# The attention's maxima: two heads as products on half the rows each

## Chip, cores, metric

The kernel runs on one core of a Trainium2 chip. The metric is the device time of one execution in microseconds. Three runs of the kernel before took 2360.37, 2365.2 and 2371.74 us; their median is 2365.2.

## The reference

One layer computes a prompt of 2048 tokens and a sample group of 8 x 4 tokens: RMSNorm, one input projection, then native sparse attention (NSA) beside a gated DeltaNet, and one output projection. What the change touches is the attention of the prompt. It has 8 query heads of 64 dimensions in 2 groups of 4; each group shares one key/value head. Three branches are softmaxed by themselves and summed under gates: compressed blocks, the 8 selected blocks of 64 keys, and a window of 512 keys.

```python
def window_banded(q, k, v):
    ...
    s = jnp.einsum('bnqhgd,bnkhd->bhgnqk', q_b, kw).astype(jnp.float32) * (NSA_HEAD_DIM ** -0.5)
    ...
    p = jax.nn.softmax(jnp.where(m, s, MASK_VALUE), axis=-1)
```

A softmax subtracts a maximum per query and head, and that maximum may be approximate, since it cancels. The selected branch does the same over the chosen blocks.

## The kernel before, in words

The program runs through input projection, gated DeltaNet (`gdn`, with the compression of keys beside it), attention (`nsa`) and output projection. A scheduler of the framework writes the order of every engine at build time: it goes through the recorded instructions by priority and by its own estimate of when operands and buffers are ready. PE, the tensor engine, then takes its products in exactly that order.

**Units.** `nsa` works in 8 units: 4 blocks of 512 queries (`qs`) times 2 groups of heads (`h`). While the scores of one unit are streamed (`stream`), `prepare` computes the maxima of the next, some of its steps after each step of the stream. For the first unit `prepare` runs alone beside the end of the DeltaNet's recurrence.

**Operands.** Queries and keys are split into a high and a low part. `QHL` [128, 4, 512] holds a group's 4 heads: rows 0 to 63 the high part (16 rotated dimensions `rh`, 48 others `qh`), rows 64 to 127 the low part (`rl`, `ql`). `KHH` holds the keys' high part twice, in rows 0 to 63 and 64 to 127. A product over all 128 rows is thus (high + low) x high. `load_q` (L1213 for each DMA) loads QHL with four DMAs on SP's queue.

**Maxima.** For each of the unit's 4 query tiles `s` and 4 heads `g`, `smax` (L1374) multiplies 128 queries with up to 512 keys into a PSUM tile `psm`, adds the causal mask of the last tile by a second product, the bf16 identity times the bf16 mask `neglow` (L1376), and VectorE reduces each 64 keys to a maximum in `bm` (L1377). `wmax` (L1389 to L1391) does this for the window into `psw`, in one or two pieces, always with a mask. `wmax0` (L1397 to L1400) takes all 4 heads at the window's far edge into `psv`. The PSUM tiles come from `pM` with 3 buffers, shared with `psc`, `psi`, `tsel`, `L`, `B` and others.

**Stream.** For each key tile and pair of heads `score` makes two products per head (L1440 on QHL's 128 rows, L1441 on 98 rows) into `pss`, ScalarE exponentiates them (L1482), and two products with the values (L1573) go to the halves of `O`: the even head to columns 0 to 63, the odd one to 64 to 127. `B` (L1528) has 24 rows. `gdn_setup` and L695 use the same bf16 identity and mask for the DeltaNet's decay.

```python
mm = nc.tensor.matmul(O[64 * gg:64 * gg + 64, c0:c1], val, W[j][gg][:, c0:c1], ..., tile_position=(0, 64 * gg))
```

`tile_position` names the first row and column of the part of the array that a product uses.

Of the kernel before, what the change touches and what calls it, by code (L numbers as in the profile page):

```python
# [104 lines left out]
class K:  # L105
# [15 lines left out]
    def setup(self):  # L121
# [3 lines left out]
        self.identb = self.const.tile([128, 128], BF16, name="identb")  # L125
        nc.vector.tensor_copy(self.identb, self.ident)
# [28 lines left out]
    def setup2(self):  # L155
        nc = self.nc
        self.masks = {}
        with self.pool(name="set", bufs=1, side="right") as sp:
            for n in ("negtri", "neglow"):
                f = sp.tile([128, 128], F32, tag="f", name="f_" + n)  # L160
                nc.sync.dma_start(f, self.i[n][:, 0:128])
                self.masks[n] = self.const.tile([128, 128], BF16, name=n)
                nc.vector.tensor_copy(self.masks[n], f)
# [399 lines left out]
    def gdn_setup(self, cp, bank):  # L563
# [6 lines left out]
        negtri = cp.tile([128, 512], BF16, name="negtri")  # L570
        nc.vector.tensor_copy(negtri, ntf)
        nc.sync.dma_start(ntf, i["headind"])
# [64 lines left out]
    def gdn(self):  # L637
        nc, tc, i, o = self.nc, self.tc, self.i, self.o
        with self.gst as st:
# [51 lines left out]
            def build(n):  # L691
# [3 lines left out]
                nc.tensor.matmul(psd, self.identb, negtri, start=True, stop=False)  # L695
# [510 lines left out]
    def nsa(self):  # L1206
        nc, tc, i, o = self.nc, self.tc, self.i, self.o
        with ExitStack() as st:
# [38 lines left out]
            def load_q(qs, h):  # L1247
# [8 lines left out]
                dma(QHL[0:16], qv(self.rh))  # L1256
                dma(QHL[16:64], qv(self.qh, 16))
                dma(QHL[64:80], qv(self.rl))
                dma(QHL[80:128], qv(self.ql, 16))
# [17 lines left out]
            def X(shape, name):  # L1277
                return pM.tile(shape, F32, tag="m", name=name)
# [10 lines left out]
            tri4 = wk.tile([128, 4, 128], BF16, name="tri4", bufs=1)  # L1289
            nc.gpsimd.tensor_copy(tri4, self.masks["negtri"].unsqueeze(1).to_broadcast([128, 4, 128]))  # L1290
# [6 lines left out]
            def prepare(u):  # L1297
# [71 lines left out]
                def smax(s, g, a):  # L1369
                    qt = 4 * qs + s  # L1370
                    b = min(a + 4, qt + 1)
                    diag = b == qt + 1
                    ps = X([128, 512], "psm")
# [3 lines left out]
                    nc.vector.tensor_reduce(out=bm[:, s, g, 2 * a:2 * b], in_=ps[:, 0:128 * (b - a)].rearrange("p (n k) -> p n k", k=64), axis=AX.X, op=ALU.max)  # L1377
                    busy["d"] += 0.1 + 0.14 * (b - a)

                def wmax(s, g):  # L1380
# [3 lines left out]
                    lhs = QHL[:, g, 128 * s:128 * s + 128]  # L1384
                    ps = X([128, 512], "psw")
                    parts = [(x, y) for x, y in ((a, min(e, 4 * qs)), (max(a, 4 * qs), e)) if x < y]
                    for x, y in parts:
                        last = y == e
                        nc.tensor.matmul(ps[:, 128 * (x - a):128 * (y - a)], lhs, key(KHH, 1, h, x, y), start=True, stop=not last)  # L1389
                    nc.tensor.matmul(ps[:, 128 * (qt - a):128 * (qt - a) + 128], self.identb, self.masks["neglow"], start=False, stop=True)  # L1390
                    nc.vector.tensor_reduce(out=ww[:, g, s, 0:1], in_=ps[:, 0:128 * (e - a)], axis=AX.X, op=ALU.max)  # L1391
                    busy["d"] += 0.1 + 0.14 * (e - a)
# [22 lines left out]
                for s in range(4):  # L1415
                    for g in range(4):
                        B += [lambda s=s, g=g, a=a: smax(s, g, a) for a in range(0, 4 * qs + s + 1, 4)]
                        B += [lambda s=s, g=g: wmax(s, g)]
# [18 lines left out]
            prepare.steps = lambda u: 16 + 32 + 16 * u["qs"] + (4 if u["qs"] else 0)  # L1437
# [615 lines left out]
```

## Time and profile before

| | |
|---|---|
| median of three runs | 2365.2 us |
| profiled execution | 2365.14 us |
| span of its trace | 2363.4 us |
| PE busy | 2183.8 us (92%) |
| VectorE (DVE) busy | 1280.0 us (54%) |
| ScalarE (ACT) busy | 796.7 us (34%) |
| GpSimd (POOL) busy | 763.3 us (32%) |
| granted clock of PE, mean | 0.958 |

PE's busy time is that of its products, whose ends are modelled and overlap; its weight loads are a row of their own (PEld). What a product costs is read from the starts of the products around it. The attention is the stretch from about 1239 to 2065 us.

### The profile page before, as it was taken

What the parts mean: (1) busy time and instruction counts of PE and PEld (TensorE: products, weight loads), DVE (VectorE), ACT (ScalarE), POOL (GpSimd) and SP (SyncE); (2) the same over time, 40 slices, a digit from 0 to 9 for tenths busy, and PEclk for the clock granted to TensorE, in tenths of its full rate; (3) what the DMA queues carried; (4) which work ended last, traced back from release to release, by engine and by line L of the source; (5) the groups of instructions that cost most, each with busy time, mean ns of one, the idle gap of its engine ahead of it and who ended that gap; (6) DMA issues with size and microseconds to landing.
All of it is one profiled execution on the core that took longest, in us unless ns stands there. A gap on an engine that the chain in (4) does not pass through costs nothing. (4 is left out here: it accounts for less than half of the span.)

```text
span 2363.4 us, 36125 instructions
## 1 busy us (share of the span) xinstructions
PE 2183.8 (92%) x13338; PEld 1668.8 (71%) x13340; DVE 1280.0 (54%) x2660; ACT 796.7 (34%) x1688; POOL 763.3 (32%) x957
## 2 busy tenths in 40 slices
PE   4999989999999899996793899999999999999998
PEld 4999888999999888996682455455455453477765
DVE  4300135566521266566551578687768787844542
ACT  4411224332214133453351324334343444522221
POOL 2104211111100004512141246455464655422742
PEclk9999999999999899998796989998999999999999
DMA  8432331124442464546638342232122102384652
GB/s 244 130 83 93 100 106 63 59 69 81 119 145 87 141 179 128 157 128 150 138 104 169 62 83 52 35 67 53 39 47 39 28 6 60 93 241 145 197 189 94
DMA packets 304467, 248.12 MB, mean 105 GB/s; under 512 B 106039, under 2 KB 260835, under 8 KB 301987
## 3 DMA queue, kind: packets, MB, share of 16 engines
q1 hardware_dynamic: 282923, 194.53, 32.2%
q0 software_dynamic: 7424, 33.56, 4.2%
q10 hardware_dynamic: 13944, 17.72, 2.6%
q8 instruction: 105, 1.72, 0.3%
q14 instruction: 71, 0.58, 0.1%
HBM read 173.60 MB, written 74.42 MB: 105 GB/s over the span
## 5 line engine op out<-in xcount | busy, mean ns | idle before, releaser
L1583 POOL TENSOR_TENSOR pt<-pt 128x512 f32<-128x512 f32 (+3 forms) x332 | 320.6, 977 | 371.4 <-DVE pt L1492 178.9
L1482 ACT ACTIVATE pt<-pss 128x512 f32<-128x512 f32 (+3 forms) x544 | 254.8, 494 | 383.9 <-PE pss L1441 204.4
L1573 PE MATMUL O<-pt,V 128*64 128x512 f32 (+3 forms) x1088 | 243.1, 527 | 10.9 <-DVE pt L1492 10.9
L1377 DVE TENSOR_REDUCE bm<-psm 128x8 f32<-128x512 f32 (+3 forms) x320 | 189.6, 603 | 66.3 <-PE psm L1374 49.5
L1440 PE MATMUL pss<-qhl,khh 128*128 128x512 f32 (+3 forms) x544 | 218.6, 407 | 1.2 <-ACT pt L1482 0.6
L1440 PEld LDWEIGHTS pss<-qhl,khh 128*128 128x128 f32 x544 | 105.4, 194 | 135.9 <-issue 97.2
L1441 PE MATMUL pss<-qhm,klm 98*128 98x512 f32 (+3 forms) x544 | 191.8, 361 | 5.4 <-DMA qhl<-rl 4.0
L261 PE MATMUL ps<-xhi,whi 128*128 128x416 f32 x880 | 191.0, 359 | 2.5 <-ACT sb L514 2.5
L261 PE MATMUL ps<-xhi,wlo 128*128 128x416 f32 x880 | 189.7, 355 | 0.0
L261 PE MATMUL ps<-xlo,whi 128*128 128x416 f32 x880 | 187.6, 354 | 0.0
L261 PEld LDWEIGHTS ps<-xhi,whi 128*128 128x128 f32 x880 | 166.7, 191 | 15.9 <-issue 4.7
L261 PEld LDWEIGHTS ps<-xlo,whi 128*128 128x128 f32 x880 | 166.1, 189 | 2.1
L261 PEld LDWEIGHTS ps<-xhi,wlo 128*128 128x128 f32 x880 | 165.7, 189 | 1.9
L1492 DVE TENSOR_TENSOR pt<-pt,caps 128x128 f32<-128x128 f32 x349 | 138.1, 415 | 21.1 <-ACT pt L1482 19.9
L1374 PE MATMUL psm<-khh,qhl 128*128 128x512 f32 (+3 forms) x320 | 129.0, 416 | 18.0 <-DMA qhl<-ql 11.5
L1583 DVE TENSOR_TENSOR pt<-pt 128x512 f32<-128x512 f32 (+3 forms) x148 | 122.8, 839 | 32.7 <-PE O L1573 17.4
L466 DVE SCALAR_TENSOR_TENSOR acc<-cx,wc,acc 128x416 f32<-128x416 f32 (+1 forms) x180 | 124.1, 690 | 4.6
L1441 PEld LDWEIGHTS pss<-qhm,klm 98*128 98x128 f32 x544 | 106.4, 197 | 17.0 <-DMA qhl<-rl 4.9
L1573 PEld LDWEIGHTS O<-pt,V 128*64 128x64 f32 x1088 | 55.9, 137 | 85.6 <-issue 33.3
L239 DVE TENSOR_TENSOR wlo<-wraw,whi 128x1024 fp32r<-128x1024 f32 x30 | 35.7, 1223 | 146.1 <-ACT whi L238 133.9
L1391 DVE TENSOR_REDUCE ww<-psw 128x1 f32<-128x512 f32 (+3 forms) x128 | 80.9, 632 | 51.7 <-PE psw L1390 50.9
L1374 PEld LDWEIGHTS psm<-khh,qhl 128*128 128x128 f32 x320 | 62.0, 198 | 57.2 <-issue 16.6
(506 smaller groups left out, 4150.3 us busy)
## 6 DMA issues: line engine op xcount, KB each, us to landing
kq<-qkvt SPq DMA_DIRECT2D x64, 256.0 KB
qkvt<-acc SPq DMA_DIRECT2D x60, 208.0 KB
wraw<-w_in SPq DMA_DIRECT2D x24, 512.0 KB
xt<-x_prompt SPq DMA_DIRECT2D x16, 512.0 KB
m<-mx SPq DMA_DIRECT2D x16, 512.0 KB
x<-x_prompt ACTq DMA_DIRECT2D x16, 512.0 KB
out<-y SPq DMA_DIRECT2D x16, 512.0 KB
qh<-hi SPq DMA_DIRECT2D x20, 208.0 KB
```

The costliest lines, as they stand in the source:

```text
L239: nc.vector.tensor_tensor(out=wlo[:, :, c:c + m], in0=raw, in1=whi[:, :, c:c + m].bitcast(F32), op=ALU.subtract)
L261: nc.tensor.matmul(ps, x, y, start=(k == 0), stop=(k == 23))
L466: nc.vector.scalar_tensor_tensor(acc[:, :n], cx[:, j:j + n], wc[:, j, c:c + 1], acc[:, :n], op0=ALU.mult, op1=ALU.add)
L1374: nc.tensor.matmul(ps[:, 0:128 * (b - a)], QHL[:, g, 128 * s:128 * s + 128], key(KHH, 0, h, a, b), start=True, stop=not diag)
L1377: nc.vector.tensor_reduce(out=bm[:, s, g, 2 * a:2 * b], in_=ps[:, 0:128 * (b - a)].rearrange("p (n k) -> p n k", k=64), axis=AX.X, op=ALU.max)
L1391: nc.vector.tensor_reduce(out=ww[:, g, s, 0:1], in_=ps[:, 0:128 * (e - a)], axis=AX.X, op=ALU.max)
L1440: nc.tensor.matmul(ps, lhs1, r1, start=True, stop=False)
L1441: nc.tensor.matmul(ps, lhs2, r2, start=False, stop=True)
L1482: last = nc.scalar.activation(pt[:, c0:c1], ps[:, c0:c1], AF.Exp)
L1492: last = nc.vector.tensor_tensor(out=x, in0=x, in1=caps[:, int(nm == "neglow")], op=ALU.min)
L1573: mm = nc.tensor.matmul(O[64 * gg:64 * gg + 64, c0:c1], val, W[j][gg][:, c0:c1], start=(n == 0), stop=(n == N - 1), tile_position=(0, 64 * ...
L1583: (nc.gpsimd if e == "p" else nc.vector).tensor_tensor(out=acc[gg][:, c0:c1], in0=acc[gg][:, c0:c1], in1=W[j][gg][:, c0:c1], op=ALU.add)
```

## The change

The rows of QHL are swapped for odd heads: even heads have the high part in rows 0 to 63 and the low part in 64 to 127, odd heads the other way round. KHH is the same in both halves, so the full products of the scores and of `wmax0` do not change. `smax` and `wmax` now take a pair of heads `p`: each head's product runs over its high part alone, 64 rows, at row 64 * j for head j of the pair, into a PSUM tile of its own. The low part of the queries is left out of these maxima. A dependency without a wait keeps the pair's products in the order odd, even. The identity and the masks are fp32r; `tri4` is replaced by a broadcast of `negtri`. QHL is loaded with eight DMAs, each for two heads. `prepare` has half as many steps for the maxima, each twice as large.

```diff
+        self.identr = self.const.tile([128, 128], F32R, name="identr")
+        nc.vector.tensor_copy(self.identr, self.ident)
...
+        for n in ("negtri", "neglow"):
+            self.masks[n] = self.const.tile([128, 128], F32R, name=n)
...
+        negtri = cp.tile([128, 512], F32R, name="negtri")
         nc.vector.tensor_copy(negtri, ntf)
+        nc.vector.tensor_copy(self.masks["negtri"], ntf[:, 0:128])
+        nc.sync.dma_start(ntf[:, 0:128], i["neglow"][:, 0:128])
+        nc.vector.tensor_copy(self.masks["neglow"], ntf[:, 0:128])
...
-                nc.tensor.matmul(psd, self.identb, negtri, start=True, stop=False)
+                nc.tensor.matmul(psd, self.identr, negtri, start=True, stop=False)
...
-                dma(QHL[0:16], qv(self.rh))
-                dma(QHL[16:64], qv(self.qh, 16))
-                dma(QHL[64:80], qv(self.rl))
-                dma(QHL[80:128], qv(self.ql, 16))
+                for odd in range(2):
+                    for a, r, x in ((64 * odd, self.rh, self.qh), (64 - 64 * odd, self.rl, self.ql)):
+                        dma(QHL[a:a + 16, odd::2], qv(r)[:, odd::2])
+                        dma(QHL[a + 16:a + 64, odd::2], qv(x, 16)[:, odd::2])
...
+                def both(name, ws, mask=None):
+                    t = [X([128, 512], name) for _ in range(2)]
+                    def run(p, s):
+                        first = None
+                        for n, (c, k) in enumerate(ws):
+                            for j in (1, 0):
+                                r = slice(64 * j, 64 * j + 64)
+                                mm = nc.tensor.matmul(t[j][:, c:c + k.shape[-1]], QHL[r, 2 * p + j, s], k[r], start=True, stop=not (mask is not None and n == len(ws) - 1), tile_position=(64 * j, 0))
+                                if first is not None:
+                                    tc.add_manual_dep(mm.ins, first.ins.name, mybir.DependencyInfo(mybir.DependencyClass.NoSync, mybir.DependencyReason.DATA), reason="both heads at once")
+                                first = mm
+                        if mask is not None:
+                            for j in (1, 0):
+                                nc.tensor.matmul(t[j][:, mask:mask + 128], self.identr, self.masks["neglow"], start=False, stop=True)
+                        return t
+                    return run
...
-                    nc.tensor.matmul(ps[:, 0:128 * (b - a)], QHL[:, g, 128 * s:128 * s + 128], key(KHH, 0, h, a, b), start=True, stop=not diag)
-                    if diag:
-                        nc.tensor.matmul(ps[:, 128 * (qt - a):128 * (qt - a) + 128], self.identb, self.masks["neglow"], start=False, stop=True)
+                    t = both("psm", [(0, key(KHH, 0, h, a, b))], 128 * (qt - a) if b == qt + 1 else None)(p, slice(128 * s, 128 * s + 128))
+                    for j in range(2):
+                        nc.vector.tensor_reduce(out=bm[:, s, 2 * p + j, 2 * a:2 * b], in_=t[j][:, 0:128 * (b - a)].rearrange("p (n k) -> p n k", k=64), axis=AX.X, op=ALU.max)
...
+                    t = both("psw", [(128 * (x - a), key(KHH, 1, h, x, y)) for x, y in parts], 128 * (qt - a))(p, slice(128 * s, 128 * s + 128))
...
-                    nc.tensor.matmul(ps, self.identb, tri4, start=True, stop=False)
+                    nc.tensor.matmul(ps, self.identr, self.masks["negtri"].unsqueeze(1).to_broadcast([128, 4, 128]), start=True, stop=False)
...
-            prepare.steps = lambda u: 16 + 32 + 16 * u["qs"] + (4 if u["qs"] else 0)
+            prepare.steps = lambda u: 16 + 16 + 8 * u["qs"] + (4 if u["qs"] else 0)
```

**The order, first place.** PE in the stream of the unit with `qs` 2 and `h` 1, while the maxima of `qs` 3, `h` 0 are made: unmasked maxima. `psm` are the maxima, `pss` the scores, `O` the values; `khh` is a block of 512 keys. Before:

```order
L1374 MATMUL psm<-khh_11699,qhl_11700 128x512
L1440 MATMUL pss<-qhl_11706,khh_11711 128x512
L1441 MATMUL pss<-qhm_11707,klm_11712 128x512
L1374 MATMUL psm<-khh_11705,qhl_11700 128x512
L1573 MATMUL O<-pt,V_11709 64x512 x2
L1440 MATMUL pss<-qhl_11706,khh_11711 128x384
L1441 MATMUL pss<-qhm_11707,klm_11712 128x384
L1374 MATMUL psm<-khh_11711,qhl_11700 128x512
```
The changed kernel, in the stream of the same unit (the lines of scores and values are 10 higher):

```order
L1376 MATMUL psm<-khh_11692,qhl_11693 128x512
L1450 MATMUL pss<-qhl_11699,khh_11692 128x512
L1451 MATMUL pss<-qhm_11700,klm_11695 128x512
L1450 MATMUL pss<-qhl_11699,khh_11692 128x512
L1451 MATMUL pss<-qhm_11700,klm_11695 128x512
L1583 MATMUL O<-pt,V_11696 64x512 x2
L1376 MATMUL psm<-khh_11692,qhl_11693 128x512
L1450 MATMUL pss<-qhl_11699,khh_11698 128x512
L1451 MATMUL pss<-qhm_11700,klm_11701 128x512
L1376 MATMUL psm<-khh_11698,qhl_11693 128x512 x2
L1450 MATMUL pss<-qhl_11699,khh_11698 128x512
```
A head's product stood alone between scores before. Now the two products of a pair stand apart, with four products of the scores and two of the values between the first two; the next pair stands together.

**The order, second place.** The same unit, maxima with a mask (`neglow`). Before:

```order
L1374 MATMUL psm<-khh_11715,qhl_11700 128x128
L1376 LDWEIGHTS identb
L1376 MATMUL psm<-neglow,identb 128x128
L1440 MATMUL pss<-qhl_11706,khh_11711 128x256
L1441 MATMUL pss<-qhm_11707,klm_11712 128x256
L1389 MATMUL psw<-khh_11711,qhl_11700 128x384
L1389 MATMUL psw<-khh_11715,qhl_11700 128x128
L1390 LDWEIGHTS identb
L1390 MATMUL psw<-neglow,identb 128x128
```
The changed kernel (the odd head of a pair, then the even one):

```order
L1376 MATMUL psm<-khh_11708,qhl_11693 128x128
L1382 MATMUL psm<-neglow,identr 128x128
L1450 MATMUL psr<-QRL,chh 128x512
L1451 MATMUL psr<-QRM,cxl 128x512
L1376 MATMUL psm<-khh_11708,qhl_11693 128x128
L1382 MATMUL psm<-neglow,identr 128x128
L1583 MATMUL O<-pt,V_11706 64x128 x2
```
and a few rows later, the window's pair:

```order
L1583 MATMUL O<-pt,V_11696 64x512 x2
L1538 MATMUL B<-R,ep 128x512
L1376 MATMUL psw<-khh_11704,qhl_11693 128x384 x2
L1376 MATMUL psw<-khh_11708,qhl_11693 128x128 x2
L1382 MATMUL psw<-neglow,identr 128x128 x2
```
Before, each product was followed by its mask. Now a masked pair of `psm` is split: product and mask of one head, two products of `psr`, product and mask of the other. The window's pair, in two pieces of 384 and 128 keys, stands together, and its two masks follow it.

## Rows read from the trace of the kernel before

**Rows 1.** Busy time of each engine by stretches (the header names the columns).
```profile
core 0: us, PE busy (x) PEld busy (x) DVE busy (x) ACT busy (x) POOL busy (x), PEclk, DMA share, GB/s
1119.80:1238.70 118.90, 104.50 (x1004) 87.99 (x1004) 69.10 (x207) 51.89 (x182) 37.91 (x63) 0.89 0.49 120
1238.70:2065.40 826.70, 753.01 (x3618) 392.24 (x3616) 600.18 (x1200) 312.77 (x664) 395.14 (x402) 0.94 0.28 59
1238.70:1400.00 161.30, 114.48 (x596) 64.01 (x596) 82.76 (x213) 40.96 (x100) 42.19 (x58) 0.85 0.54 109
1800.00:2065.40 265.40, 255.55 (x1175) 123.94 (x1173) 213.00 (x386) 117.78 (x241) 140.09 (x129) 0.97 0.18 45
```
**Rows 2.** PE's groups by line, 1238.7 to 2065.4 us.
```profile
L1440 PE MATMUL pss<-qhl,khh 128*128 128x512 f32 (+3 forms) x544 | 218.6, 407 | 1.2 <-ACT pt L1482 0.6
L1374 PE MATMUL psm<-khh,qhl 128*128 128x512 f32 (+3 forms) x304 | 121.9, 414 | 17.1 <-DMA qhl<-ql 11.5 <-DVE ww L1391 3.7 <-DVE bm L1377 1.6
L1389 PE MATMUL psw<-khh,qhl 128*128 128x128 f32 (+3 forms) x184 | 51.1, 342 | 0.7 <-DVE ww L1391 0.2
L1376 PE MATMUL psm<-neglow,identb 128*128 128x128 bf16 x112 | 26.3, 235 | 0.0
```
**Rows 3.** Who waited for whom, PE and its weight loads (PEld), same stretch: us, times, longest.
```profile
PE psr L1441 <- DMA QRM<-rows: 32.8, 1, 32.8
PE psm L1374 <- DMA qhl<-ql: 11.5, 6, 4.1
PEld pss L1440 <- ACT pt L1482: 31.2, 57, 0.8
PEld psm L1374 <- DVE bm L1377: 15.0, 25, 1.7
```
**Rows 4.** PE in order of time: start us, length us, then the instruction; scores and maxima.
```profile
1511.46 0.40 PE L1440 MATMUL pss<-qhl,khh 128*128 128x512 f32 x1
1511.69 0.40 PE L1441 MATMUL pss<-qhm,klm 98*128 98x512 f32 x1
1511.93 0.39 PE L1374 MATMUL psm<-khh,qhl 128*128 128x512 f32 x1
```
**Rows 5.** PE in order of time around a product on 24 rows.
```profile
1437.48 0.39 PE L1374 MATMUL psm<-khh,qhl 128*128 128x256 f32 x1
1437.71 0.23 PE L1376 MATMUL psm<-neglow,identb 128*128 128x128 bf16 x1
1437.75 0.48 PE L1440 MATMUL psr<-QRL,chh 128*128 128x512 f32 x1
1438.07 0.39 PE L1441 MATMUL psr<-QRM,cxl 98*128 98x512 f32 x1
1438.39 0.49 PE L1528 MATMUL B<-R,ep 24*128 24x512 f32 x1
1438.81 0.50 PE L1440 MATMUL pss<-qhl,khh 128*128 128x512 f32 x1
1439.14 0.40 PE L1441 MATMUL pss<-qhm,klm 98*128 98x512 f32 x1
1439.39 0.28 PE L1389 MATMUL psw<-khh,qhl 128*128 128x256 f32 x1
```
**Rows 6.** PE in order of time, from transposes to a product on 64 rows and 64 columns.
```profile
932.66 0.60 PE L1161 MATMUL tp<-ident,subh 128*128 128x128 f32 x4
932.99 0.27 PE L1161 MATMUL tp<-ident,subh 128*128 128x128 f32 x1
933.19 0.67 PE L777 MATMUL pq<-Y,A 64*64 64x64 f32 x8
```
**Rows 7.** PE in order of time, values: two heads on column halves.
```profile
1509.88 1.08 PE L1573 MATMUL O<-pt,V 128*64 128x512 f32 x4
1510.36 0.60 PE L1573 MATMUL O<-pt,V 128*64 128x512 f32 x2
1510.89 0.50 PE L1440 MATMUL pss<-qhl,khh 128*128 128x512 f32 x1
```
**Rows 8.** SP's issues of line 1213: length of one, shortest, median, longest, in ns.
```profile
L1213 SPq DMA_DIRECT2D qhl<-ql x8: 302/424/427, 1103.1 to 1824.2; - x8
```

More of the change, by code (lines that the diff above doesn't have):

```diff
@@ L124, in setup @@
         nc.sync.dma_start(self.ident, self.i["ident"])
-        self.identb = self.const.tile([128, 128], BF16, name="identb")
-        nc.vector.tensor_copy(self.identb, self.ident)
+        self.identr = self.const.tile([128, 128], F32R, name="identr")
+        nc.vector.tensor_copy(self.identr, self.ident)
         self.ones = self.const.tile([128, 128], F32, name="ones")
@@ L157, in setup2 @@
         self.masks = {}
[L158 to L163, printed above, removed]
+        for n in ("negtri", "neglow"):
+            self.masks[n] = self.const.tile([128, 128], F32R, name=n)
         self.ovl = self.const.tile([128, 32], F32, name="ovl")
@@ L569, in gdn_setup @@
         nc.sync.dma_start(ntf, i["negtri"])
-        negtri = cp.tile([128, 512], BF16, name="negtri")
+        negtri = cp.tile([128, 512], F32R, name="negtri")
         nc.vector.tensor_copy(negtri, ntf)
+        nc.vector.tensor_copy(self.masks["negtri"], ntf[:, 0:128])
+        nc.sync.dma_start(ntf[:, 0:128], i["neglow"][:, 0:128])
+        nc.vector.tensor_copy(self.masks["neglow"], ntf[:, 0:128])
         nc.sync.dma_start(ntf, i["headind"])
@@ L1288, in nsa @@
             busy = {"p": 0.0, "d": 0.0}
-            tri4 = wk.tile([128, 4, 128], BF16, name="tri4", bufs=1)
-            nc.gpsimd.tensor_copy(tri4, self.masks["negtri"].unsqueeze(1).to_broadcast([128, 4, 128]))
             caps = wk.tile([128, 2, 128], F32, name="caps", bufs=1)
@@ L1367, in sel_rows @@
                     nc.sync.dma_start(QHM[64:96, 1:4].bitcast(F32), QHM[64:96, 0:1].bitcast(F32).to_broadcast([32, 3, 512]))
-                def smax(s, g, a):
+                def both(name, ws, mask=None):
[14 more added lines that the diff above has]
+                    return run
@@ L1370, in smax @@
+                def smax(s, p, a):
                     qt = 4 * qs + s
                     b = min(a + 4, qt + 1)
-                    diag = b == qt + 1
-                    ps = X([128, 512], "psm")
-                    nc.tensor.matmul(ps[:, 0:128 * (b - a)], QHL[:, g, 128 * s:128 * s + 128], key(KHH, 0, h, a, b), start=True, stop=not diag)
-                    if diag:
-                        nc.tensor.matmul(ps[:, 128 * (qt - a):128 * (qt - a) + 128], self.identb, self.masks["neglow"], start=False, stop=True)
@@ L1377, in smax @@
-                    nc.vector.tensor_reduce(out=bm[:, s, g, 2 * a:2 * b], in_=ps[:, 0:128 * (b - a)].rearrange("p (n k) -> p n k", k=64), axis=AX.X, op=ALU.max)
-                    busy["d"] += 0.1 + 0.14 * (b - a)
-                def wmax(s, g):
+                    t = both("psm", [(0, key(KHH, 0, h, a, b))], 128 * (qt - a) if b == qt + 1 else None)(p, slice(128 * s, 128 * s + 128))
+                    for j in range(2):
+                        nc.vector.tensor_reduce(out=bm[:, s, 2 * p + j, 2 * a:2 * b], in_=t[j][:, 0:128 * (b - a)].rearrange("p (n k) -> p n k", k=64), axis=AX.X, op=ALU.max)
@@ L1382, in wmax @@
+                    busy["d"] += 2 * (0.1 + 0.14 * (b - a))
+                def wmax(s, p):
                     qt = 4 * qs + s
                     a, e = max(0, qt - 3), qt + 1
-                    lhs = QHL[:, g, 128 * s:128 * s + 128]
-                    ps = X([128, 512], "psw")
                     parts = [(x, y) for x, y in ((a, min(e, 4 * qs)), (max(a, 4 * qs), e)) if x < y]
-                    for x, y in parts:
-                        last = y == e
-                        nc.tensor.matmul(ps[:, 128 * (x - a):128 * (y - a)], lhs, key(KHH, 1, h, x, y), start=True, stop=not last)
@@ L1390, in wmax @@
-                    nc.tensor.matmul(ps[:, 128 * (qt - a):128 * (qt - a) + 128], self.identb, self.masks["neglow"], start=False, stop=True)
-                    nc.vector.tensor_reduce(out=ww[:, g, s, 0:1], in_=ps[:, 0:128 * (e - a)], axis=AX.X, op=ALU.max)
-                    busy["d"] += 0.1 + 0.14 * (e - a)
+                    t = both("psw", [(128 * (x - a), key(KHH, 1, h, x, y)) for x, y in parts], 128 * (qt - a))(p, slice(128 * s, 128 * s + 128))
+                    for j in range(2):
+                        nc.vector.tensor_reduce(out=ww[:, 2 * p + j, s, 0:1], in_=t[j][:, 0:128 * (e - a)], axis=AX.X, op=ALU.max)
@@ L1394, in wmax0 @@
+                    busy["d"] += 2 * (0.1 + 0.14 * (e - a))
                 def wmax0(s):
@@ L1415, in prepare @@
                 for s in range(4):
-                    for g in range(4):
-                        B += [lambda s=s, g=g, a=a: smax(s, g, a) for a in range(0, 4 * qs + s + 1, 4)]
-                        B += [lambda s=s, g=g: wmax(s, g)]
+                    for p in range(2):
+                        B += [lambda s=s, p=p, a=a: smax(s, p, a) for a in range(0, 4 * qs + s + 1, 4)]
+                        B += [lambda s=s, p=p: wmax(s, p)]
                     if qs:
```

## The prediction

> **What bounds the kernel now.** I read the windows of the stage first. The attention with its maxima is the stretch from 1238.7 to 2065.4 us: TensorE (PE) is busy 753.0 of 826.7 us, VectorE 600.2, ScalarE 312.8, GpSimd 395.1; in its last third PE is busy 255.6 of 265.4 us [rows 1]. So this stage goes at PE's pace, and PE takes its products strictly in the written order. The maxima are 520 products of queries with keys here (160 pairs of heads for psm, 100 for psw); the 304 + 184 of them in this stage, with their masks, are among PE's larger groups [rows 2]. Of PE's 73.7 us of idle time 32.8 are a single wait for a DMA, another 11.5 wait for the load of QHL, and the rest are short waits for ScalarE and VectorE [rows 3].
>
> The durations in PE's rows overlap, so a product's price is read from starts. In a run of products that all use the whole array, 512 columns follow each other at 0.23 us: 1511.46, 1511.69, 1511.93 [rows 4]. Call the part of the array that a product takes its layout (128, 64 or 32 rows; 128, 64 or 32 columns). **Where the layout changes the pace breaks.** B has 24 rows: psr starts 0.32 us before it instead of 0.23, B itself lasts 0.42 until the next start, and the first product after it 0.33, before the pace is back at 0.25 with the next [rows 5]. So a change first costs 0.09 us (the running product must end before anything of the new layout starts) and then 0.10 us more in the new layout (0.42 against 0.32, 0.33 against 0.23: the first weights are not loaded under the product before). Together 0.19 us per change to a layout of 128 weight columns; into O's 64 columns about half of the load, 0.14. A change to 64 rows is in the trace too, with 64 columns: four transposes start from 932.66 to 932.99, 0.11 apart, then 0.20 pass until pq [rows 6]. That is the same 0.09.
>
> **The change, part by part.**
>
> *Side by side.* The 520 products stream 198,656 columns (counted in the order), before and after. A product on 64 rows costs as much as one on 128, unless the partner on the other half runs at the same time. The trace shows column halves side by side: four products of O in 1.01 us, two of them in 0.53 [rows 7]. Row halves at 128 columns it doesn't show; bounds: full overlap or none. In the order of the changed kernel, though, the two heads mostly do not stand together: the dependency fixes that odd comes before even, not that nothing comes between. Scores, values and masks stand between them, as both places of the order above show. The half-row products form 370 stretches; 274 hold one product alone, 55 two, 28 three, 13 four. Only 41,472 columns have a partner. At 0.23 us per 512 columns that saves 18.6 us at most, 0 at least; I take 18.6, since O's halves overlap fully.
>
> *Layout changes.* Before, the maxima were whole-array products like the scores (pss) around them and changed nothing. Now each stretch is entered and left. I counted the changes of layout in the order: 672 in the stage before, 1224 after, 552 more, of them 543 to 128 weight columns. 543 x 0.19 + 9 x 0.14 = 104 us. From below: if weights for half the rows can load while other products run, only the 0.09 is left, 50 us; if a change between 128 and 64 rows at 128 columns is free, 0. From above 0.19, as B's rows are the nearest (128 columns, fewer rows). I take 104.
>
> *Masks.* 256 masks take fp32r weights instead of bf16. The bf16 mask costs 0.04 us until the next start and leaves the next load bare, 0.32 instead of 0.23 [rows 5]: 0.13. An fp32r mask of 128 columns is paced by its load, 0.11 like the transposes [rows 6]; 214 of the 256 follow a half-row product, and their bare load is already in the price of the change. So 0, with -5 to +8 as bounds (256 x -0.02 to +0.03). The 24 masks of psv and 16 of psd stand behind 512-column products that hide a load of 0.11: 0.
>
> *DMA.* QHL is loaded with 8 DMAs instead of 4 of the same bytes; an issue takes 0.42 us on SP [rows 8]. PE already waits 11.5 us in six times for QHL's last piece [rows 3], and four more issues ahead of it are up to 1.7 us in seven loads: 0 to 12, I take 2, since in the new order other products stand ahead of the first maximum. The two mask copies from ntf, and tri4's copy that falls away on GpSimd, have no follower on PE's path in this stage: 0.
>
> *Before the stage.* From 1119.8 to 1238.7 the first maxima run beside the end of the recurrence; PE is busy 104.5 of 118.9 us [rows 1] at small chained products. The changes of layout grow from 97 to 156 there: 59 x 0.19 = 11 us at most; the chain sets the end, I take 3.
>
> *Buffers.* A pair holds two of pM's three PSUM buffers. VectorE has 227 us to spare in the stage [rows 1], and PE waits 15.0 us for psm's reductions now [rows 3]. A slower PE leaves them more time, so no new wait is counted.
>
> **The sum.** In the stage 104 - 19 = +85 us of PE at the full clock. The granted clock is 0.94 [rows 1], so +91. Of the 41 us of idle time that are not the one long wait, a slower PE can swallow some, at most all; I take 12. With 3 and 2 that is +84 us. The profiled execution took 2365.1 us, the median of the runs is 2365.2, so nothing is to be corrected: **2449 us**.
>
> **The rivals.**
>
> *Free changes (faster).* Place: the step from a whole-array product to a half-row one and back. If a 64 x 128 half starts and ends like a whole-array product, the 552 changes cost nothing, and -19 / 0.94 + 5 gives 2350. It decides where a change costs under 0.03 us (19 / 552). For it: no row shows exactly this layout. Against: the pauses for 24 rows [rows 5] and for 64 rows with 64 columns [rows 6] are equal, and no change in the rows I read is free. Chance 0.08. The Trainium skill (TensorEngine Tiling (Array Packing), Theoretical Speedup) gives up to 2x for a contraction of at most 64 rows; taken for every pair that would be 198,656 / 2 columns or 45 us, and 2320. The order speaks against it, with partners for 41,472 columns, and the same page's Key Properties say that a change of mode drains the engine, which the trace shows as 0.09 us.
>
> *Half the price (less slow).* The load of the new layout's weights runs under the product before, and only 0.09 us remains: 552 x 0.09 = 50, -19, / 0.94 = +33, -12 +5 gives 2391. For it: the halves are separate rows. Against: B's 24 rows are as separate and pay 0.10 for the load [rows 5]. Chance 0.12. The Trainium skill (TensorE: Matmul & The Clock Gate, Part 3: Packing small matmuls) says that weight loads overlap running products only where the row groups differ. A half shares its rows with the whole-array product before it, so by that rule the load stays bare; B's rows agree.
>
> *Swallowed (no change).* If PE's idle time and the waits behind its overlapping rows took up the +91, the time would stay within 12 us of 2365. For it: 41 us of idle time. Against: in the last third 10 of 265 us are idle [rows 1]. Chance 0.06.
>
> *The clock falls.* Not a case of its own, but it sets the upper end: in the first part of the stage, with PE busy 114.5 of 161.3 us, the granted clock was 0.85 [rows 1]. If more pauses bring the stage from 0.94 to 0.90, some 840 us of work grow by 4.4%, 37 us; without the overlap come 20 more.
>
> **How the numbers follow.** The forecast has 0.74, the rivals 0.08, 0.12 and 0.06. A measurement of this kernel can tell about 0.5%, 12 us, from no change. Faster: 0.08. The same: 0.06. Slower: 0.74 + 0.12 = 0.86. The range runs from 2385, just below the half price, to 2495, the forecast with part of the fallen clock and no overlap.
>
> **What would show it.** Right: a lone half-row psm of 512 columns with about 0.32 us before it, 0.42 until the next start and 0.33 after; pairs that stand together start some ns apart; the stage some 85 us longer; VectorE's and ScalarE's busy time the same; the granted clock near 0.94. Wrong: half-row products at 0.23 us on either side (free changes), or 0.32 in place of 0.42 (half the price); then the stage is equal or shorter. If the stage grows while those starts stay close, the wait would be at the reductions (psm for bm) or QHL's load.

## The result, and the profile after the change

The changed kernel takes **2452.4 us** (median of 4 runs, 2447.39 to 2469.35) against 2365.9 us before in the same runs: a ratio of 1.0388, with a 95% interval of 1.035 to 1.0427. It is slower by 87 us; 2449 was predicted. Its profiled execution took 2449.35 us, with a span of 2447.6 us.

The windows of the changed kernel, cut at the same events as [rows 1] (first psm, first pss, the stage, its first and last parts):

```profile
core 0: us, PE busy (x) PEld busy (x) DVE busy (x) ACT busy (x) POOL busy (x), PEclk, DMA share, GB/s
1108.10:1227.30 119.20, 116.73 (x1000) 93.50 (x1000) 70.75 (x207) 52.34 (x182) 37.29 (x64) 0.91 0.48 119
1227.30:2149.00 921.70, 868.17 (x3616) 420.41 (x3616) 596.86 (x1216) 310.59 (x664) 378.76 (x386) 0.90 0.23 53
1227.30:1400.00 172.70, 130.44 (x516) 70.34 (x514) 68.23 (x176) 37.01 (x89) 31.01 (x46) 0.74 0.45 93
1883.60:2149.00 265.40, 259.62 (x1060) 116.47 (x1061) 191.05 (x338) 109.80 (x223) 128.17 (x114) 0.95 0.17 45
```

The stage takes 921.7 us instead of 826.7, which is +95. PE's busy time in it grows by 115 us; VectorE's (600.2 to 596.9) and ScalarE's (312.8 to 310.6) do not. The last third of the same length holds 1060 products instead of 1175. The stretch ahead of the stage is as long as before (119.2 against 118.9), though PE is busy for 12 us more in it. And the granted clock of the stage is 0.90, where it was 0.94. The stage begins 11.4 us earlier than before (1227.3 against 1238.7), and 9 of these lie ahead of the first products of the projections on whole weight tiles, which start at 245.9 instead of 255.0 us. So the sum is +95 and -11.

The groups of PE by line in the stage answer to [rows 2]:

```profile
L1450 PE MATMUL pss<-qhl,khh 128*128 128x512 f32 (+3 forms) x544 | 229.1, 426 | 1.1 <-ACT pt L1492 0.9
L1376 PE MATMUL psm<-khh,qhl 64*128 64x512 f32 (+3 forms) x304 | 124.4, 490 | 2.3 <-DMA qhl<-qh 1.6 <-ACT rows L1285 0.4
L1376 PE MATMUL psw<-khh,qhl 64*128 64x128 f32 (+3 forms) x184 | 48.4, 403 | 0.0
L1382 PE MATMUL psm<-neglow,identr 128*128 128x128 f32 x112 | 39.5, 353 | 0.0
```

The same 304 + 184 products now say 64*128, half the rows. One psm lasts 490 ns instead of 414, although some of them run beside a partner, and the scores (pss), which nobody touched, grow from 407 to 426: they now more often stand first behind a change of layout, and the clock is lower. The waits for qhl fell from 11.5 us in six times [rows 3] to 1.6.

PE in order of time shows the price of one change. First a lone half-row product between scores, then two that stand together (x2), then a lone one with its mask:

```profile
1566.68 0.50 PE L1450 MATMUL pss<-qhl,khh 128*128 128x512 f32 x1
1567.02 0.40 PE L1451 MATMUL pss<-qhm,klm 98*128 98x512 f32 x1
1567.35 0.50 PE L1376 MATMUL psm<-khh,qhl 64*128 64x512 f32 x1
1567.78 0.50 PE L1450 MATMUL pss<-qhl,khh 128*128 128x512 f32 x1
1568.12 0.40 PE L1451 MATMUL pss<-qhm,klm 98*128 98x512 f32 x1
...
1601.94 0.40 PE L1451 MATMUL pss<-qhm,klm 98*128 98x512 f32 x1
1602.27 0.50 PE L1376 MATMUL psm<-khh,qhl 64*128 64x512 f32 x2
1602.70 0.65 PE L1583 MATMUL O<-pt,V 128*64 128x256 f32 x4
...
1604.33 0.40 PE L1451 MATMUL pss<-qhm,klm 98*128 98x512 f32 x1
1604.66 0.44 PE L1376 MATMUL psm<-khh,qhl 64*128 64x384 f32 x1
1605.02 0.33 PE L1382 MATMUL psm<-neglow,identr 128*128 128x128 f32 x1
1605.28 0.32 PE L1376 MATMUL psw<-khh,qhl 64*128 64x128 f32 x1
```

The lone product starts 0.33 us behind the score ahead of it, the next score 0.43 behind it, the one after that 0.34 later: the 0.32, 0.42 and 0.33 that the prediction took from B [rows 5]. In a run without changes each of the three would be 0.23 [rows 4]. The pair takes 0.33 and 0.43 as well, for two heads instead of one. So an excursion (into the half rows and back) costs 1.10 - 0.69, some 0.4 us, twice the 0.19 of the sum and a little more; a pair saves 0.23 and pays the same. The mask of 128 columns pays less: it starts at 1605.02 and the next product at 1605.28, 0.26 later, of which 0.09 are the next change's; the other 0.17 are 0.06 above its pace of 0.11 [rows 6], where the sum has 0.10.

The Trainium skill (TensorE: Matmul & The Clock Gate, Part 3: Packing small matmuls) says that weight loads overlap running products only where the row groups differ. Behind a change of layout the trace agrees, with 0.43 and 0.34 where a running layout has 0.23 and only 0.10 more ahead of the change. Within one layout it does not: the weight loads of the scores last 187 ns at the median, for the same 128 rows as the products before them, and still these products follow each other at 0.23 us [rows 4]. What the trace shows bare is the first load behind a change.

```profile
L1450 PEld LDWEIGHTS pss<-qhl,khh x544: 186/187/334, 1227.3 to 2146.3; 128*128 128x128 f32 x182
```

### The profile page after: what moved, and what is told of

Same layout as the page of the kernel before. It is cut to its first block, busy times and chain, and to the rows that moved or that the text cites. A ratio compares the mean times of both kernels' runs of the same rounds, so it can differ in the third digit from the quotient of the medians.

```text
span 2447.6 us, 36135 instructions
## 1 busy us (share of the span) xinstructions
PE 2311.2 (94%) x13340; PEld 1704.7 (70%) x13340; DVE 1278.7 (52%) x2676; ACT 795.2 (32%) x1688; POOL 746.7 (31%) x940
## 5 line engine op out<-in xcount | busy, mean ns | idle before, releaser
L1593 POOL TENSOR_TENSOR pt<-pt 128x512 f32<-128x512 f32 (+3 forms) x314 | 303.0, 978 | 452.5 <-PE O L1583 195.0
L1583 PE MATMUL O<-pt,V 128*64 128x512 f32 (+3 forms) x1088 | 252.4, 539 | 10.1 <-DVE pt L1502 9.9
L1450 PE MATMUL pss<-qhl,khh 128*128 128x512 f32 (+3 forms) x544 | 229.1, 426 | 1.1 <-ACT pt L1492 0.9
L1502 DVE TENSOR_TENSOR pt<-pt,caps 128x128 f32<-128x128 f32 x347 | 126.0, 380 | 67.9 <-ACT pt L1492 66.3
L1376 PE MATMUL psm<-khh,qhl 64*128 64x512 f32 (+3 forms) x320 | 131.1, 488 | 3.1 <-DMA qhl<-qh 1.6
L1376 PEld LDWEIGHTS psm<-khh,qhl 64*128 64x128 f32 x320 | 53.9, 194 | 81.9 <-issue 30.1
```

The costliest lines, as they stand in the source:

```text
L1376: mm = nc.tensor.matmul(t[j][:, c:c + k.shape[-1]], QHL[r, 2 * p + j, s], k[r], start=True, stop=not (mask is not None and n == len(ws) - ...
L1450: nc.tensor.matmul(ps, lhs1, r1, start=True, stop=False)
L1502: last = nc.vector.tensor_tensor(out=x, in0=x, in1=caps[:, int(nm == "neglow")], op=ALU.min)
L1593: (nc.gpsimd if e == "p" else nc.vector).tensor_tensor(out=acc[gg][:, c0:c1], in0=acc[gg][:, c0:c1], in1=W[j][gg][:, c0:c1], op=ALU.add)
```

## The experiments

Two columns of the table need a word. The product of span and granted clock (medians over the runs) is the length that the span would have at the full 2.4 GHz if all in it went by TensorE's clock; waits are counted too, so it is a yardstick, good to some 5 us. What is left of the span is "lost to the clock". Each ratio is to runs of the kernel before on the same chip, whose median was 2365 to 2368 us; its row is from the runs beside e1_whole to e4_pairs.

| kernel | us | ratio to before (95%) | clock | span x clock | lost |
|---|---|---|---|---|---|
| before | 2367.0 | 1 | 0.955 | 2259 | 106 |
| changed | 2452.4 | 1.0388 (1.035 to 1.0427) | 0.9435 | 2313 | 138 |
| e1_whole | 2358.3 | 0.9956 (0.9936 to 0.9977) | 0.958 | 2259 | 99 |
| e2_masks | 2367.2 | 0.9989 (0.9974 to 1.0005) | 0.952 | 2252 | 113 |
| e3_samehalf | 2538.5 | 1.0673 (1.0616 to 1.0729) | 0.916 | 2324 | 213 |
| e4_pairs | 2474.9 | 1.0434 (1.04 to 1.0467) | 0.9245 | 2286 | 187 |
| e5_rows66 | 2404.2 | 1.0164 (1.0123 to 1.0204) | 0.9385 | 2255 | 148 |
| e6_values4 | 2373.1 | 1.0031 (1.0007 to 1.0055) | 0.949 | 2250 | 121 |
| e7_values4_ahead | 2371.8 | 1.0003 (0.9985 to 1.002) | 0.9485 | 2249 | 122 |
| e8_rows96 | 2380.3 | 1.0074 (1.0055 to 1.0092) | 0.952 | 2264 | 114 |
| e9_psm_half | 2425.7 | 1.0246 (1.0216 to 1.0276) | 0.948 | 2298 | 126 |
| e10_nested | 2356.2 | 0.9965 (0.9951 to 0.9979) | 0.9545 | 2248 | 107 |

**Are the half rows the cost? (e1_whole)**

```diff
-                                r = slice(64 * j, 64 * j + 64)
-                                mm = nc.tensor.matmul(..., tile_position=(64 * j, 0))
+                                r = slice(0, 128)
+                                mm = nc.tensor.matmul(...)
```

> The changed kernel in which the maxima's products take all 128 rows again (high and low part, as before the change); pairs, their order, their two PSUM buffers, the eight QHL loads and the fp32r masks stay. Counted in its order: 680 changes of layout in the stage (672 before the change, 1224 after). Theory (a change to 128 weight columns costs 0.19 us): the stage is back at 827 us, and what the changed kernel gained ahead of 255 us (some 11 us) stays: 2354 us, granted clock in the stage back at 0.94. Rival (the pair's two buffers, its order or the loads cost the time, not the half rows): it stays near 2440 us, and the stage near 915.

Measured 2358.3 us. The pairs, their two buffers, the eight loads and the fp32r masks are all still there, and the whole loss is gone; the rival's 2440 is out. Its windows, the stage and a stretch in its middle:

```profile
1230.10:2052.50 822.40, 752.45 (x3618) 406.82 (x3616) 594.12 (x1216) 308.88 (x664) 378.66 (x386) 0.95 0.27 60
1400.00:1787.00 387.00, 376.73 (x1863) 208.23 (x1862) 301.58 (x612) 152.57 (x327) 205.90 (x210) 0.99 0.24 53
```

PE's busy time, 752.5 us, is that of the kernel before (753.0). This version is faster than the changed kernel by 94 us and than the kernel before by 0.4%.

**The masks alone (e2_masks).** The kernel before with identr and the fp32r masks copied from ntf; tri4 and the pool "set" fall away.

> The kernel before with the new masks and identity alone: fp32r, copied from the recurrence's own mask tile, so that two loads of masks at the start fall away; products of the maxima and loads of QHL as before. Theory: the first 255 us get about 11 us shorter as in the changed kernel, since in both the first weights' loads stand ahead of the copies of the window caches, and the masks cost nothing that shows: 2354 us, and e1_whole within 5 us of it. Rival (fp32r masks cost): a mask lasts 0.16 us until the next start in place of 0.04, 256 x 0.12 = 31 us, so 2385 us. Second rival (the 11 us belong to the pairs, not to the masks' setup): 2366 us or more, and PE's first products wait 16 us for their weights as before.

Measured 2367.2 us: neither 2354 nor 2385. The part ahead of the stage gets shorter, but by less than the 11 us that were expected: the first psm starts at 1110.6 instead of 1119.8, the first pss at 1232.2 instead of 1238.7. The stage is longer:

```profile
1232.20:2070.80 838.60, 766.97 (x3616) 419.43 (x3616) 601.51 (x1200) 311.05 (x664) 393.42 (x402) 0.92 0.28 59
```

It takes 12 us more than before, at a clock of 0.92 instead of 0.94; times the clock it is no longer (772 against 777 us). The same masks in e1_whole go with a stage of 822 us at 0.95. So 31 us for the masks are excluded; whether the 6 us between the ratios of e2_masks and e10_nested (below, bf16 masks) belong to the masks, to the clock or to the other order of the products stays open.

**Is the partner worth anything? (e3_samehalf)**

```diff
-                                r = slice(64 * j, 64 * j + 64)
-                                mm = nc.tensor.matmul(..., tile_position=(64 * j, 0))
+                                r = slice(0, 64)
+                                mm = nc.tensor.matmul(..., tile_position=(0, 0))
```

> The changed kernel with both heads' products on rows 0 to 63 (QHL loaded as before the change), so none has a partner on the other half; the same values are computed. Counted: 1206 changes of layout in the stage, 40,704 columns without the partner that they have in the changed kernel. Theory (partners run fully side by side): 40,704 x 0.23 / 512 = 18 us, less 18 x 0.19 = 3 us for fewer changes, at the clock of 0.90 some +17 us: 2469 us. Rival (side by side gives nothing in the end, since the next change waits for both): 2449 us.

Measured 2538.5 us, some 70 more than the theory. Span times clock says what happened: it grew by 11 us (2313 to 2324; 15 expected), but 213 us are lost to the clock instead of 138. The stage, and PE around two heads' products that stand together on the same half:

```profile
1233.70:2240.10 1006.40, 943.07 (x3617) 457.38 (x3616) 598.71 (x1216) 311.20 (x664) 378.74 (x386) 0.84 0.23 49
...
1709.82 0.40 PE L1451 MATMUL pss<-qhm,klm 98*128 98x512 f32 x1
1710.15 0.73 PE L1376 MATMUL psm<-khh,qhl 64*128 64x512 f32 x2
1710.81 0.50 PE L1450 MATMUL pss<-qhl,khh 128*128 128x512 f32 x1
```

On the same half the two take 0.66 us (1710.15 to 1710.81), on two halves 0.43 (1602.27 to 1602.70 above). So partners do run side by side. The rest of the 70 us is the clock, 0.84 with PE busy for 94% of the time; why it falls so far here stays open (below).

**Would pairs held together pay? (e4_pairs)**

```diff
+                                if first is None and back:
+                                    tc.add_manual_dep(mm.ins, back[0].name, ...Sync...)
...
+                                mk = nc.tensor.matmul(t[j][:, mask:mask + 128], self.identr, ...)
+                                tc.add_manual_dep(mk.ins, first.ins.name, ...NoSync...)
...
+                    with tc.high_priority(offset=60):
+                        f(*a)
```

("back" holds the last reduction of the pair before; f is smax or wmax.)

> The changed kernel with the two heads' products held together: a pair's first product waits until the pair before it is reduced, so that two buffers are free, and the masks stand behind both products. Counted: 989 changes of layout in the stage in place of 1224, 89,984 columns with a partner in place of 40,704. Theory: 235 x 0.19 = 45 us and 49,280 x 0.23 / 512 = 22 us less, 67 us at the full clock, some 73 at 0.92: 2379 us, with up to 5 us less again ahead of the stage. Rival (waits for the reductions take the place of the changes, since a pair now holds two of three buffers from its first product until both reductions are over): the granted clock and PE's busy share fall, PE waits for bm and ww, and the time stays above 2430 us.

Measured 2474.9 us: the rival, slower even than the changed kernel. The pairs do stand together and cost what a lone product did, as PE in order of time shows:

```profile
1702.40 0.39 PE L1461 MATMUL pss<-qhm,klm 98*128 98x512 f32 x1
1702.72 0.50 PE L1377 MATMUL psm<-khh,qhl 64*128 64x512 f32 x2
1703.16 0.50 PE L1460 MATMUL pss<-qhl,khh 128*128 128x512 f32 x1
1703.49 0.40 PE L1461 MATMUL pss<-qhm,klm 98*128 98x512 f32 x1
```

0.32, 0.44 and 0.33 for both heads. Span times clock falls by 26 us against the changed kernel, not by 67, and 49 us more are lost to the clock. Window of the stage, and PE's waits in it:

```profile
1223.30:2178.70 955.40, 853.32 (x3618) 414.23 (x3616) 606.09 (x1216) 306.85 (x664) 378.32 (x386) 0.84 0.23 52
```

```profile
PE psm L1377 <- DVE bm L1395: 15.3, 16, 1.4
PE psw L1377 <- DVE bm L1395: 6.8, 10, 1.3
PE psm L1377 <- DVE ww L1406: 5.7, 9, 1.2
```

PE is idle for 102 us of the stage instead of 54: 28 us wait for the reductions of the pair before, and other waits grow behind them. Of the gain of 67 us that was expected, the longer idle time took 48 and the lower clock 49, together more than all of it.

**Pauses or rows: what does the clock go with? (e5_rows66, e8_rows96).** Both kernels differ from e3_samehalf in the rows alone: 66 or 96 of 128 rows have the layout of the whole array, so the maxima bring no pauses.

```diff
-                                r = slice(0, 64)
-                                mm = nc.tensor.matmul(..., tile_position=(0, 0))
+                                r = slice(0, 66)
+                                mm = nc.tensor.matmul(...)
```

> As e3_samehalf, but a product takes rows 0 to 65 (the high part and two rows of the low part), so it has the layout of the whole array: 683 changes of layout in the stage (e1_whole 680, changed kernel 1224), while only about half the rows are at work in the maxima, as in the changed kernel. Span times granted clock was 2259 us for the kernel before and for e1_whole, 2313 for the changed kernel; the rest of the span, lost to the clock, was 106, 99 and 138 us. Theory now (the pauses at the changes lower the granted clock, as they add to what the changes cost): no pauses, so the clock stays at 0.958 and the time is e1_whole's, 2358 us. Rival (the clock falls because only half the rows work): the lost time is the changed kernel's, 138 us, without its pauses: 2259 + 138 + 2 = 2399 us, clock 0.942. In both, the price of the changes (0.19 us) predicts span times clock of 2259 us.

Measured 2404.2 us, clock 0.9385: the rival. The clock falls without any more pauses, so my theory that they are what lowers it fell. That they have no part in it is not shown: e3_samehalf, with 64 rows, the same loads of QHL and 523 more changes, loses 213 us to the clock, this kernel 148. The other half of the expectation held: with no more changes than e1_whole, span times clock is 2255 against 2259. The windows answer to e1_whole's two:

```profile
1226.30:2098.00 871.70, 791.85 (x3616) 430.95 (x3616) 592.76 (x1216) 310.66 (x664) 377.60 (x386) 0.89 0.26 56
1400.00:1832.00 432.00, 417.44 (x1925) 231.62 (x1924) 313.55 (x648) 157.36 (x335) 209.30 (x216) 0.91 0.24 49
```

In the middle of the stage PE is busy for 96.6% of the time (417.4 of 432.0), in e1_whole for 97.3%; the granted clock is 0.91 against 0.99. The kernels differ in the rows of 520 products and in the loads of QHL (four here, eight in e1_whole), and 49 us of lost clock go with that.

> As e5_rows66, with rows 0 to 95 (the high part and half of the low part): 679 changes of layout in the stage, no more pauses than e1_whole. With all rows e1_whole lost 99 us of its span to the clock, with 66 rows e5_rows66 lost 148, at the same span times clock (2259 and 2255 us). Theory (the fewer rows at work, the lower the granted clock): half way, 124 us lost, 2382 us. Rival (the fall of e5_rows66 has another cause that comes with any product on fewer rows, such as its changed order): 2404 us. Third (three quarters of the rows are enough): 2358 us.

Measured 2380.3 us, between the other two, with 114 us lost (99, 148). But that does not show 96 rows half way. The kernels whose maxima use all rows lose between 99 (e1_whole) and 122 us (e7_values4_ahead), and 114 lies among them; 148 does not. The stage, a stretch in its middle, and PE's wait for QHL:

```profile
1229.20:2078.30 849.10, 764.00 (x3616) 415.03 (x3616) 594.97 (x1216) 310.14 (x664) 378.25 (x386) 0.93 0.27 58
1400.00:1812.90 412.90, 394.45 (x1928) 217.22 (x1929) 317.42 (x652) 156.60 (x335) 209.84 (x217) 0.98 0.25 51
...
PE psm L1376 <- DMA qhl<-ql: 13.0, 4, 5.0
```

The clock in the middle is 0.98, close to e1_whole's 0.99, and half of the 22 us between the two kernels is a longer wait for QHL (13.0 us; 2.1 in e1_whole). What is shown is that with the same loads 66 rows lose 34 us more to the clock than 96.

**Does the cost follow the changes? (e9_psm_half)**

```diff
-                                r = slice(64 * j, 64 * j + 64)
+                                r = slice(64 * j, 64 * j + 64) if name == "psm" else slice(0, 128)
```

> The changed kernel with half rows for psm alone; the window's products (psw) take the whole array, high and low part, as in e1_whole. Counted: 1065 changes of layout in the stage (changed kernel 1224, e1_whole 680), 27,776 columns with a partner (40,704). Theory (the changes carry the cost, whatever product makes them, and the clock goes with the half rows): the changes are 385 of 544 more, or 71 percent, and so are the half-row columns; 2358 + 0.7 x 94 = 2424 us. Rival (psw carries most of it, as it has two products and always a mask behind them): under 2400 us.

Measured 2425.7 us against 2424 (the runs lie between 2416.7 and 2450.2): 72% of the cost (67.4 of 94.1 us) for 71% of the changes. The half-row columns are 70% as well (139,264 of 198,656), so this run rules out that the window's products carry most of it, but cannot tell changes from columns. That the changes cost the time rests on the starts of the products above.

**What came off ahead of 255 us? (e10_nested)** In e10_nested, what setup2 does behind the masks is called inside their "with" block:

```diff
                 nc.vector.tensor_copy(self.masks[n], f)
+            self.setup3()
+
+    def setup3(self):
+        nc = self.nc
         self.ovl = self.const.tile([128, 32], F32, name="ovl")
```

> The kernel before with one move: the pool of the page table opens inside the pool of the masks and so has its own place, and need not wait until the masks' pool is given back; bf16 masks and all else as before. In its order the page table's loads now stand at the head of ScalarE's queue, ahead of the copies of the window caches, as in the changed kernel. Theory (the copies ran ahead of the first weights and delayed them by 12 us): PE's 16 us wait for the first weights goes and the time falls by 8 to 9 us: 2357 us. Rival (the gain ahead of 255 us in the changed kernel comes from the two mask loads that fell away): 2366 us.

Measured 2356.2 us. Rows of SP's and ScalarE's queues show the way. Before:

```profile
1.25 0.76 ACTq L1204 DMA_DIRECT2D out<-cache_win_k  x1
2.19 15.19 SPq L236 DMA_DIRECT2D wraw<-w_in  x2
```

In the changed kernel:

```profile
0.80 2.62 ACTq L167 DMA_DIRECT2D pti<-page_table  x4
2.26 4.04 SPq L232 DMA_DIRECT2D wraw<-w_in  x2
15.70 0.64 ACTq L1203 DMA_DIRECT2D out<-cache_win_k  x1
```

And in e10_nested:

```profile
2.25 4.15 SPq L240 DMA_DIRECT2D wraw<-w_in  x2
```

Before, the copies of the window caches are issued at 1.25 us, ahead of the first weights, whose two issues then take 15.19 us on SP; PE waits for those weights:

```profile
PE ps L249 <- ACT whi L238: 16.1, 1, 16.1
```

With the page table at the head of ScalarE's queue the copies come at 15.7 us (17.7 in e10_nested) and the weights' issues take 4.04 (4.15). The page table could not go first before because its pool waited for the masks' pool "set"; the changed kernel has no such pool any more. The two mask loads themselves are not it: e10_nested still makes them. Why the issues are slow behind the copies is not shown; that they are slow in that order and not in the other is. Nor do all 9 us lie at one place: in e10_nested the first products on whole weight tiles start at 250.6, 4 us earlier than before, the first psm at 1108.0, 12 us earlier.

**The price on another product (e6_values4, e7_values4_ahead).** If a change costs 0.19 us, fewer of those that were always there should pay. O's products of two key tiles are held back until both are ready:

```diff
+                    held.append((j, k, b, p, n, N, x))
+                    if N > 1 and n % 2 == 0:
...
+                    for (j, k, b, p, n, N, x) in held:
...
+                            if gg == 0 and len(held) == 2 and j == held[0][0]:
+                                tc.add_manual_dep(mm.ins, W[held[1][0]][2].ins.name, ...Sync...)
```

> e1_whole, with the products of the values (O, 64 columns) of two key tiles held back until both tiles are through ScalarE and masked, so that four of them stand together instead of two: 459 changes of layout in the stage instead of 680. Theory (the prices of the prediction hold for any change): 127 fewer into narrow layouts x 0.14 + 94 fewer into 128 columns x 0.19 = 36 us less, and no more loss to the clock than e1_whole's 99 us: 2322 us or less. Rival (a new wait: the first tile's products now wait for the second tile's scores, ScalarE and mask, with three score buffers): PE waits for pt and pss, the clock falls, and the time is 2358 us or more.

> As e6_values4, with the scores running two key tiles ahead of the values instead of one: 462 changes of layout in the stage. Theory (only the changes count): the same time as e6_values4, 2322 us. Rival (the waits for the second tile eat the gain of e6_values4): faster than e6_values4 by the waits of PE's O products for pt that its profile shows.

Measured 2373.1 and 2371.8 us: no gain, the time and the clock of e6_values4's rival. The stage of e6_values4, and PE's wait of its O products, behind it that of e1_whole:

```profile
1237.20:2082.60 845.40, 757.13 (x3617) 436.15 (x3616) 610.04 (x1226) 306.81 (x664) 376.92 (x377) 0.91 0.25 58
...
PE O L1591 <- DVE pt L1502: 10.8, 12, 4.2
PE O L1583 <- DVE pt L1502: 11.3, 12, 4.2
```

Span times clock fell by 9 us against e1_whole (2259 to 2250) instead of 36, and 22 us more are lost to the clock. PE is idle for 88 us of the stage (e1_whole 70) and its clock is 0.91 (0.95). The wait for the second tile, the rival's mechanism, is not what ate the gain: O's products wait for pt no longer than in e1_whole, and scores that run two tiles ahead change nothing. What did is open. Whether shorter groups or more score buffers would keep the gain was not tried.

## Why the prediction was right, and where it was not

The time came out 3 us from the forecast, but its parts did not: 24 us less of work than forecast, 26 us more lost to the clock. That the sum fits is luck: two errors of nearly the same size cancel.

**What bounds the stage: right.** VectorE and ScalarE kept their busy times, and the time followed PE's work, its waits and its clock.

**The price of a change: right at long products.** 0.32, 0.42 and 0.33 were forecast around a lone product; 0.33, 0.43 and 0.34 are in the trace. e1_whole shows that the half rows carry the whole loss. In sum the price was set too high: against e1_whole, where only the rows differ, span times clock grows by 54 us, while the 85 of the sum less 16 us of idle time (69.9 in e1_whole, 53.5 here) would be 69. By the mask's 0.06 in place of 0.10 above, 214 masks behind half-row products make some 8 of these 15 us, an estimate; the rest is open. The rivals "free changes" and "half the price" needed other starts than these, and are out.

**Side by side: right in size, but not for the reason given.** Pairs that stand together take the time of one, and there are as few of them as the order said. Without partners span times clock grew by 11 us, where the terms gave 15. But the row behind "O's halves overlap fully" does not show a gain: two of O's products start together, and the next two 0.48 us later (1509.88 and 1510.36 [rows 7]), no sooner than two whole-array products one behind the other (0.47: 1511.46 to 1511.93 [rows 4]). By that row the term would have been 0 and the forecast 20 us higher; that the two row halves do better than the two column halves was luck. That most pairs would not meet was read rightly from the order; e4_pairs shows that making them meet does not by itself repair the loss.

**Masks: 0 within some 6 us**, as said; e2_masks leaves the rest open.

**QHL's loads: wrong in sign, small.** "0 to 12, I take 2"; in fact the wait fell by 10 us (11.5 to 1.6), and in e1_whole, with the same eight loads, it was 2.1 us. The split seems to help: kernels with eight loads waited 1.6 to 5.2 us, those with four 7.2 to 13.0, except e3_samehalf (2.6).

**Idle time swallowed: 20 instead of 12**, the 10 us of that wait among them (73.7 us idle before, 53.5 after).

**Before the stage: half right.** The stretch got 0.3 us longer, at a clock of 0.91 instead of 0.89: some 3 us more work, as forecast, that the clock gave back. But I read no further forward than the first psm, and so missed that the pool "set" falls away in setup2 and the order of ScalarE's queue with it: 9 us less, as e10_nested shows, whose one move changes that order.

**The clock: the failed step.** The sum divided by a clock of 0.94 that it took as given, +6 us. It fell to 0.90 in the stage; over the span the loss grew from 106 to 138 us, +32. The case stood in the text as the upper end only ("if more pauses bring the stage from 0.94 to 0.90"), and its reason, more pauses, is at best a part: e5_rows66 has no more of them than e1_whole and loses 49 us more, with 66 rows. e1_whole shows that the fall comes with the half-row products. How much of it their few rows, their pauses, the missing partners or the new order make is not shown: e6_values4, with all rows at work, has a clock of 0.91 in the stage too.

Put together: the 85 us of the sum, less 20 of idle time and 9 at the start, with 3 ahead of the stage, are 59 us of work at the full clock, against 78 forecast and 54 measured (2259 to 2313); the clock took 32 against 6. 54 + 32 = 86 us, the forecast 84.

## What to carry to other kernels

Packing two small products side by side pays only for stretches that are long against two changes of layout: here a stretch cost 0.4 us for going there and back and a pair of 512 columns saves 0.23, so by these numbers even a perfect pairing of single pairs loses. Count the stretches in the order that the scheduler really made, since the two halves of a pair need not meet in it. And treat the granted clock as part of the sum: multiply span by clock before and after, so that a saving in work and a loss of clock are seen apart; e4_pairs saved 26 us of work against the changed kernel and lost 49 of clock.

## What the runs showed of the hardware that was not expected

Two products on the two row halves of the array take the time of one: a pair of 512 columns 0.43 us, two on the same half 0.66 (e3_samehalf). Two products of 512 columns on the two column halves (O) start together too, but take 0.48 us a pair [rows 7], as long as two in a row.

The granted clock can fall with the rows that products use, at the same layout and nearly the same busy share. With 66 rows for 520 products that hold about a tenth of the stage's time on PE (198,656 columns at 0.23 us per 512 are 89 us) 148 us of the span were lost to the clock, with 96 rows and the same loads 114, which is also what kernels with all 128 rows lose (99 to 122). With 64 rows, no partner and 523 more changes of layout it was 213; with 64 rows on alternating halves and as many changes, the changed kernel, 138. No single one of these causes puts the runs in order. The stage was at 2.4 GHz for most of the time and fell to 1.2 GHz in stretches; the lowest clock was always at its start (0.74 in the changed kernel up to 1400 us, and 0.74 in e6_values4 with all rows), where PE stands still for some 30 us and then has few products.

And the place of DMAs that nobody waits for can be worth 9 us: with the copies of the window caches issued at 1.25 us on ScalarE's queue, the issues of the first weights on SP's queue lasted 15.19 us, with the copies at 15.7 us 4.04.
